# Hybrid attention and RWKV-7 layer on one core: x requested one column set ahead and paced differently, the first block's second half of x loaded among the first transfers

## The chip, the core and the metric

The program runs on one core of one Trainium2 chip. The metric is the time of one execution on the device, in microseconds (us). In the texts PE is the matrix engine TensorE, DVE is VectorE, ACT is ScalarE, POOL is GpSimd, and SP is the engine that here issues nearly all DMAs.

## What is computed

One layer over 4096 tokens of width 1024, all in float32. One input projection of the normalised x feeds two groups of heads; their gated outputs are projected back, added to x, and normalised once more.

```python
xn = rms_norm(x, norm_g, RMS_EPS)
proj = xn @ w_in                          # 1024 -> 4224 columns
o_a = diff_attention(q1, q2, k1, k2, v_a, lam)          # block-causal, 4 heads
o_a = rms_norm(o_a, subln_g) * (1 - lam_init) * silu(g_a)
rwkv_in = token_shift(proj[..., 2048:], shift_mu)
r, k_b, v_b, wd, ad = split(rwkv_in)
y = rwkv7_recurrence(r, decay(wd), k_mod, v_b, kk, a(ad))   # state 64 x 64, 8 heads
o_b = (group_norm(y) + bonus) * silu(g_b)
h = x + concat([o_a, o_b]) @ w_out
out = rms_norm(h, final_g, RMS_EPS)
```

## The kernel before, in words

There are three phases: the projection together with the whole recurrence (some 2135 us of the profiled execution), the attention, and the output projection. The change touches the first phase only.

**Blocks and column sets.** The tokens are cut into eight blocks of 512. For one block x stands transposed in SBUF, as a rounded part `xh` and a remainder `xl`, and the columns of `w_in` go by in sets. Sets of group B (called r: V, two of R, two of K, the LoRA columns, the gate) and sets of group A (called a: V, two of Q, two of K, the gate) are separate runs over a block, in the order r0 a0 r1 a1 r2 a2 r3 r4 r5 r6 r7 a7 a6 a5 a4 a3. The block of x changes eleven times in that list; the last set of a run whose successor has another block carries the number of that block as `nxt`. Each run begins and ends with a token-major set (kind "t": V and the gate); the sets between are feature-major (kind "f").

**A step.** The generator `tile_job` (L340) gives one step per `yield`; a step is `mm3` (L247 to L250), three matmuls of 128x512: high times high, high times low, low times high. A t set is two parts of 16 steps. In `tm_part` (L264) one part computes two groups of 128 tokens, s0 and s0+1, over eight k; s0+1 runs two steps of k behind s0. The eight weight tiles of a t set lie in a ring of eight (`wb`); the second part frees each tile where s0+1 has used it (`release`, L241), and `prep` (L225) at once requests the tile eight places on. In the first run over a set the tile is loaded raw (L212 to L222), split into a high and a low part by ACT and DVE (L236, L237), and stored to `ws_d` (L239); later runs load it from there (L233, 512 KB a tile).

**x of the next block.** A block of x has two halves of 256 tokens, each loaded by two DMAs of 512 KB (`x_load`, L148) into `xv`, of which there are two buffers, so one half at a time. ACT sums the squares and scales (`x_norm`, L157); PE transposes in four groups of eight (`x_trans`, L168), each into a PSUM buffer `pg`, of which there are three that the recurrence shares; ACT writes `xh` (L179) and DVE `xl` (L180). Half 0 of the next block is requested at the start of the last set, normalised at step 10 of its first part, and transposed at steps 1, 4, 7 and 10 of its second part; step 11 requests half 1. Half 1 is normalised at step 4 of the first part of the next set and transposed at steps 6, 8, 10 and 12. `paced` (L322) holds these step numbers. In the first block half 1 is requested after half 0's transposes (L400), since the buffers are the same; after it, `xfree` lets raw weight tiles use the `xv` buffers (as `xr`).

**What sets the order.** PE's order in phase 1 is written by hand: a `tick` after every step advances four side streams of the recurrence (two that prepare a unit of 256 tokens, one for its chain of chunks, one for its output), each by numbers in `W` that tell after how many steps it goes on. A negative number also holds it until the next multiple of four steps. `a8` stands between the product `rk` on POOL (L506) and the matmuls `pbn` that use it (L524). The order of the other engines, SP with its DMAs among them, is made by a scheduler.

Of the kernel before, what the change touches and what calls it, by code (L numbers as in the profile page):

```python
# [27 lines left out]
    xw=2048, cw=512, pl=1, pelat=330, tb=3, pb=3, lag2=2.0, ms=40, a0=2, a1=2, a2=2, a3=2,  # L28
    a4=2, a5=2, a6=2, a7=2, a8=2, a9=2, b0=2, b1=2, b2=2, b3=2, b4=2, b5=2,
    b6=2, b7=2, b8=1, b9=1, c0=10, c1=8, c2=2, c3=2, c4=1, c5=1, c6=2, c7=3,  # L30
# [78 lines left out]
def _phase1(ctx, tc, nc, e):  # L109
# [36 lines left out]
    xraw = {}  # L146

    def x_load(b, t):  # L148
        xs = []
        for s in range(2):  # L150
            r0 = b * BT + t * 256 + s * 128
            xv = xp.tile([128, D], F32, tag="xv", name="xv", bufs=2)
            nc.sync.dma_start(xv, x[r0:r0 + 128, :])
            xs.append(xv)
        xraw[b, t] = xs
# [38 lines left out]
    def raw_next():  # L194
        while True:
# [10 lines left out]
            raw_load(n, raw)  # L206
            wr[n] = raw

    def raw_load(n, raw):
# [53 lines left out]

    def tm_part(n0, s0, evac, last, side_x):  # L264
        po = {}
        order = []
        for n in range(KD + 2):
            if n < KD:
                order.append((s0, n))
            if n >= 2:  # L270
                order.append((s0 + 1, n - 2))
        for s, k in order:
# [67 lines left out]
    def tile_job(i, kind, parts, evs, nxt):  # L340
# [5 lines left out]
        half1 = bg.pop(1, None)  # L346
        assert half1 is None or nxt is None
        if nxt is not None:
            x_load(nxt, 0)
        if half1 is not None:  # L350
            side = paced(x_half1(half1), (4, 6, 8, 10, 12, 13))
        else:
            side = paced(x_norm0(nxt) if nxt is not None else iter(()), (10,))
        yield from tm_part(n0, 0, evs[0], False, side)
        for _ in side:
            pass
        side = paced(x_half0(nxt) if nxt is not None else iter(()), (1, 4, 7, 10, 11))
        yield from tm_part(n0, 2, evs[0], True, side)
        for _ in side:
# [37 lines left out]
    def main():  # L397
        x_norm(0, 0)
        yield from x_trans(0, 0)
        x_load(0, 1)  # L400
        bg[1] = 0
        for _ in range(RING):
            prep()
        for i, (k, parts, evs, nxt, rdone) in enumerate(jobs):
            yield from tile_job(i, k, parts, evs, nxt)
            if rdone:
                done_r[0] += 1
# [1044 lines left out]
```

## Time and profile before

| what | value |
|---|---|
| median of 3 runs | 3769.85 us (3767.56 to 3772.0) |
| the profiled execution | 3761.58 us, span 3759.9 us |
| PE busy | 3609.4 us, 96% of the span |
| DVE, ACT, POOL busy | 70%, 51%, 20% |
| granted PE clock, mean of the span | 0.983 |
| DMA | 593.60 MB, mean 158 GB/s |

An engine is idle before an instruction when that one waits; the profile names who ended the wait. Matmuls are pipelined, so a busy PE is not PE at its peak, but time in which PE waits is lost unless something else bounds the stretch. The granted clock is 1.00 at 2.4 GHz and 0.50 at 1.2 GHz; a stretch of mean 0.76 was thus at the lower level for about half its time.

### The profile page before, as it was taken

How to read it: one execution, taken by the hardware profiler on the slowest of the kernel's cores; microseconds unless marked ns; L12 is line 12 of the kernel's file. 1: busy time of each engine (PE TensorE's matmuls, PEld its weight loads, DVE VectorE, ACT ScalarE, POOL GpSimd, SP SyncE). 2: the span in 40 equal slices, each digit the busy share in tenths (PEclk: the TensorE clock that was granted, in tenths of full speed). 3: DMA queues.
4: the chain of work that ended last, by engine and by line, in shares of the span. 5: the costliest groups of instructions: out<-in, count | busy, mean ns of one | idle time of the engine just before them, and what ended most of it. 6: DMA issues, size and time to landing. Idle time of an engine off the chain costs nothing.

```text
span 3759.9 us, 69957 instructions
## 1 busy us (share of the span) xinstructions
PE 3609.4 (96%) x26370; PEld 3050.9 (81%) x26370; DVE 2632.4 (70%) x5882; ACT 1922.4 (51%) x4042; POOL 761.2 (20%) x1156
## 2 busy tenths in 40 slices
PE   7999999999999999998999999999999999989999
PEld 5777777777777778777777789999999999978887
DVE  3566666667767787757777588898898898863333
ACT  4452352444445443444444377787787787761111
POOL 0112211211212222212221032222222222211000
PEclk9999999999999999999999999999999999999999
DMA  7976665666555565665675651141141131033332
GB/s 231 354 267 204 209 212 198 222 204 225 192 192 190 191 226 174 215 209 196 221 239 200 204 122 48 41 113 37 49 104 49 38 82 40 21 134 121 134 134 74
DMA packets 346092, 593.60 MB, mean 158 GB/s; under 512 B 55193, under 2 KB 210329, under 8 KB 345754
## 3 DMA queue, kind: packets, MB, share of 16 engines
q1 hardware_dynamic: 344602, 587.62, 48.4%
q8 instruction: 208, 3.41, 0.4%
q10 hardware_dynamic: 1152, 1.51, 0.1%
q14 instruction: 130, 1.06, 0.1%
HBM read 434.85 MB, written 154.14 MB: 157 GB/s over the span
## 4 chain that ended last, share of the span: by engine, by line
PE 75%; DVE 13%; DMA 4%; ACT 3%; issue 2%; SPq 2%; POOL 1%; DVEq 0%; POOLq 0%; ACTq 0%
PE po L1222 12%; PE ps L1127 6%; PE ps L1126 6%; PE tp L1197 6%; PE pjf L248 5%; PE pjf L250 4%; PE pjf L249 4%; PE pjt L248 4%; PE pjt L250 4%; PE pjt L249 4%; PE po L1372 3%; PE po L1371 3%; PE po L1370 3%; DVE DG L578 2%; DVE TL L579 2%
## 5 line engine op out<-in xcount | busy, mean ns | idle before, releaser
L1159 ACT ACTIVATE ring<-ring,nm 128x2048 f32<-128x2048 f32 (+14 forms) x472 | 589.0, 1253 | 31.3 <-DVE nm L1151 30.2
L1141 DVE CUSTOM_DVE_ANT_0 ring<-ps,zcol 128x1024 f32<-128x1024 f32 (+6 forms) x464 | 485.2, 1058 | 109.2 <-PE ps L1127 103.1
L1222 PE MATMUL po<-v,pt 128*128 128x128 f32 x4224 | 539.5, 276 | 10.0 <-ACT pt L1210 5.4
L1222 PEld LDWEIGHTS po<-v,pt 128*128 128x128 f32 x4224 | 517.9, 192 | 28.5 <-ACT pt L1210 7.3
L1126 PE MATMUL ps<-k,ta 128*128 128x512 f32 (+3 forms) x1152 | 483.1, 420 | 7.3 <-DMA ta<-q_d 4.9
L248 PE MATMUL pjt<-w,xh 128*128 128x512 f32 x1024 | 436.2, 426 | 29.1 <-DMA w<-ws_d 13.4
L248 PE MATMUL pjf<-xh,w 128*128 128x512 f32 x1088 | 451.1, 415 | 6.0 <-ACT w L236 4.5
L1127 PE MATMUL ps<-k,tb 128*128 128x512 f32 (+3 forms) x1152 | 432.0, 379 | 0.0
L250 PE MATMUL pjf<-xh,w 128*128 128x512 f32 x1088 | 431.0, 396 | 0.5 <-DVE w L237 0.5
L249 PE MATMUL pjf<-xl,w 128*128 128x512 f32 x1088 | 429.9, 395 | 0.0
L249 PE MATMUL pjt<-w,xh 128*128 128x512 f32 x1024 | 410.5, 401 | 0.9 <-DVE w L237 0.9
L250 PE MATMUL pjt<-w,xl 128*128 128x512 f32 x1024 | 410.0, 401 | 0.1
L1182 DVE SCALAR_TENSOR_TENSOR ring<-ring,rho 128x512 f32<-128x512 f32 (+3 forms) x600 | 407.1, 702 | 1.6
L1210 ACT COPY pt<-tp 128x512 f32<-128x512 f32 (+3 forms) x576 | 303.1, 550 | 194.0 <-PE tp L1197 188.7
L1197 PE MATMUL tp<-ident,ring 128*128 128x128 f32 x2112 | 313.6, 274 | 3.7 <-DVE ring L1182 3.7
L1197 PEld LDWEIGHTS tp<-ident,ring 128*128 128x128 f32 x2112 | 254.6, 142 | 40.6 <-issue 3.7
L248 PEld LDWEIGHTS pjt<-w,xh 128*128 128x128 f32 x1024 | 199.0, 194 | 80.9 <-DMA w<-ws_d 20.3
L248 PEld LDWEIGHTS pjf<-xh,w 128*128 128x128 f32 x1088 | 207.3, 191 | 57.4 <-ACT w L236 6.5
L250 PEld LDWEIGHTS pjf<-xh,w 128*128 128x128 f32 x1088 | 207.0, 190 | 49.2 <-DVE w L237 2.7
L1126 PEld LDWEIGHTS ps<-k,ta 128*128 128x128 f32 x1152 | 219.2, 190 | 32.8 <-issue 5.0
L1127 PEld LDWEIGHTS ps<-k,tb 128*128 128x128 f32 x1152 | 220.1, 191 | 23.4
L249 PEld LDWEIGHTS pjf<-xl,w 128*128 128x128 f32 x1088 | 208.0, 191 | 38.1
(205 smaller groups left out, 6421.4 us busy)
## 6 DMA issues: line engine op xcount, KB each, us to landing
w<-ws_d SPq DMA_DIRECT2D x448, 512.0 KB, 5.3
ws_d<-w SPq DMA_DIRECT2D x64, 512.0 KB, 5.3
xv<-in_x_dram SPq DMA_DIRECT2D x48, 512.0 KB, 5.4
ta<-q_d SPq DMA_DIRECT2D x128, 128.0 KB, 2.9
tb<-q_d SPq DMA_DIRECT2D x128, 128.0 KB, 3.0
k<-k_d SPq DMA_DIRECT2D x32, 512.0 KB, 7.1
mi<-mix_d SPq DMA_DIRECT2D x32, 512.0 KB, 3.3
xi<-in_x_dram SPq DMA_DIRECT2D x32, 512.0 KB, 4.2
```

Source lines behind the costliest of these rows:

```text
L248: nc.tensor.matmul(po, ah, bh, start=(k == 0), stop=False)
L249: nc.tensor.matmul(po, ah, bl, start=False, stop=False)
L250: nc.tensor.matmul(po, al, bh, start=False, stop=(k == KD - 1))
L1126: nc.tensor.matmul(ps[:, c:c + w], rr(ta[:, m, qs]), rr(k[:, m, c:c + w]), start=True, stop=False)
L1127: nc.tensor.matmul(ps[:, c:c + w], rr(tb[:, m, qs]), rr(k[:, m, c:c + w]), start=False, stop=True)
L1141: nc.vector.tensor_tensor_reduce(rg(m, ro, x), st["ps", b, m][:, c - 1024 * b:c - 1024 * b + x], msk, 0.125, -3.0e38, ALU.add, ALU.max, ac ...
L1159: nc.scalar.activation(rg(m, ro, x), rg(m, ro, x), AF.Exp, bias=st["nm"][:, m:m + 1], accum_out=st["lp"][:, m, j:j + 1])
L1182: nc.vector.scalar_tensor_tensor(rg(0, ro, x), in0=rg(1, ro, x), scalar=st["rho"], in1=rg(0, ro, x), op0=ALU.mult, op1=ALU.add)
L1197: nc.tensor.transpose(tp[:, j], rg(0, c, 128), ident)
L1210: nc.scalar.copy(pt[:, :n], st.pop(("tp", g))[:, :n])
L1222: nc.tensor.matmul(st["po"], pt[:, j], vt[h, kb // 8][:, kb % 8], start=(kb == 0), stop=(kb == i))
L1370: nc.tensor.matmul(po, mh[:, k], wh[k][:, fs], start=(k == 0), stop=False)
```

## The change

Six edits. (1) The next block's half 0 is requested before the set ahead of the last one, if the last set's weights are not fresh ones; it is then normalised at step 3, else at step 10 as before. (2) Half 0 is transposed at steps 0, 3, 5 and 8 of the second part and half 1 requested at step 9. (3) Half 1 of a later block is normalised at step 5 of the next set and transposed at steps 12, 14, 17 and 20, so the last two groups fall into the second part. (4) In the second part s0+1 runs four k behind s0 where it ran two. (5) The first block's half 1 is requested right after the fourth raw weight tile, into a buffer of the recurrence (`ARF`, first used by it later). (6) `a8` is 5 where it was 2.

```diff
-    a4=2, a5=2, a6=2, a7=2, a8=2, a9=2, b0=2, b1=2, b2=2, b3=2, b4=2, b5=2,
+    a4=2, a5=2, a6=2, a7=2, a8=5, a9=2, b0=2, b1=2, b2=2, b3=2, b4=2, b5=2,
...
-    def x_load(b, t):
+    def x_load(b, t, home=None):
...
-            xv = xp.tile([128, D], F32, tag="xv", name="xv", bufs=2)
+            xv = xp.tile([128, D], F32, tag="xv", name="xv", bufs=2) if home is None else home[:, s]
...
             raw_load(n, raw)
             wr[n] = raw
+            if n == 3:
+                home = rp.tile([128, 4, 4, 2, 64], F32, tag="ARF", name="xv1", bufs=2)
+                x_load(0, 1, home.rearrange("p (s a) b c d -> p s (a b c d)", s=2))
...
-    def tm_part(n0, s0, evac, last, side_x):
+    def tm_part(n0, s0, evac, last, side_x, lag):
...
-        for n in range(KD + 2):
+        for n in range(KD + lag):
             if n < KD:
                 order.append((s0, n))
-            if n >= 2:
-                order.append((s0 + 1, n - 2))
+            if n >= lag:
+                order.append((s0 + 1, n - lag))
...
+        if half1 is not None:
+            side = paced(x_half1(half1), (5, 12, 14, 17, 20, 21) if half1 else (4, 6, 8, 10, 12, 13))
+        elif nxt is not None:
+            if (nxt, 0) not in xraw:
+                x_load(nxt, 0)
+                side = paced(x_norm0(nxt), (10,))
+            else:
+                side = paced(x_norm0(nxt), (3,))
+        else:
+            side = iter(())
+        yield from tm_part(n0, 0, evs[0], False, side, 2)
         if nxt is not None:
-            x_load(nxt, 0)
-        if half1 is not None:
-            side = paced(x_half1(half1), (4, 6, 8, 10, 12, 13))
-        else:
-            side = paced(x_norm0(nxt) if nxt is not None else iter(()), (10,))
-        yield from tm_part(n0, 0, evs[0], False, side)
-        for _ in side:
-            pass
-        side = paced(x_half0(nxt) if nxt is not None else iter(()), (1, 4, 7, 10, 11))
-        yield from tm_part(n0, 2, evs[0], True, side)
+            for _ in side:
+                pass
+            side = paced(x_half0(nxt), (0, 3, 5, 8, 9))
+        yield from tm_part(n0, 2, evs[0], True, side, 4)
...
-        x_load(0, 1)
         bg[1] = 0
...
+            if i + 1 < len(jobs) and jobs[i + 1][3] is not None and not tiles[min(first_tile[i + 1], len(tiles) - 1)][3]:
+                x_load(jobs[i + 1][3], 0)
             yield from tile_job(i, k, parts, evs, nxt)
```

Three places show what this does to the engines' orders. The first is **SP at the start of the program**, before: `xv_213` and `xv_215` are half 1 of the first block, and the first `xr` tiles (L222) come 23 places after it, behind the small constants and the first loads of the recurrence.

```order
L239 DMA ws_d_70<-w_245 128x1024
L140 DMA lng_519<-in_ln_x_g_dram 64x256
L140 DMA lnb_522<-in_ln_x_b_dram 64x256
L153 DMA xv_213<-in_x_dram 128x1024
L153 DMA xv_215<-in_x_dram 128x1024
L140 DMA lnb_522<-in_ln_x_b_dram 64x256
L135 DMA w0h_525<-in_w0_dram 64x4x1 x2
```

And of the change (its lines are numbered from 1 to 9 higher; `xv1_139`, half 1, now stands eighth, between the fourth and the fifth raw tile):

```order
L242 DMA ws_d_70<-w_236 128x1024
L140 DMA lnb_521<-in_ln_x_b_dram 64x256
L242 DMA ws_d_70<-w_240 128x1024
L242 DMA ws_d_70<-w_244 128x1024
L225 DMA xr_351<-in_w_in_dram 128x2x64 x8
L225 DMA xr_360<-in_w_in_dram 128x2x64 x7
L317 DMA vb_d_67<-st_336 128x512
```

The first 15 of the `xr` requests moved up, directly behind the stores of the first eight tiles and ahead of most constants.

The second is **SP where block 3 gives way to block 4** (the end of r3 and the start of r4), before: `xv_8635` and `xv_8637` are half 1 of block 4, `xv_9787` and `xv_9789` are already half 0 of block 5, `w` are weight tiles, `st` evicted results. Of the eight tiles of the new set, four are requested ahead of half 1 (the last of them is the first row), four behind it.

```order
L233 DMA w_8616<-ws_d_70 128x1024
L153 DMA xv_8635<-in_x_dram 128x1024
L153 DMA xv_8637<-in_x_dram 128x1024
L233 DMA w_8633<-ws_d_70 128x1024
L233 DMA w_8649<-ws_d_70 128x1024
L233 DMA w_8654<-ws_d_70 128x1024
L314 DMA gb_d_68<-st_8642 128x512
L233 DMA w_8663<-ws_d_70 128x1024
L314 DMA gb_d_68<-st_8659 128x512
L153 DMA xv_9787<-in_x_dram 128x1024
L314 DMA vb_d_67<-st_8879 128x512
L153 DMA xv_9789<-in_x_dram 128x1024
```

And of the change (`xv_8626` is half 1 of block 4, `xv_9698` and `xv_9700` half 0 of block 5):

```order
L236 DMA w_8605<-ws_d_70 128x1024
L153 DMA xv_8624<-in_x_dram 128x1024
L153 DMA xv_8626<-in_x_dram 128x1024
L236 DMA w_8622<-ws_d_70 128x1024
L236 DMA w_8638<-ws_d_70 128x1024
L236 DMA w_8643<-ws_d_70 128x1024
L317 DMA gb_d_68<-st_8631 128x512
L236 DMA w_8648<-ws_d_70 128x1024
L236 DMA w_8653<-ws_d_70 128x1024
L236 DMA w_8662<-ws_d_70 128x1024
L317 DMA gb_d_68<-st_8658 128x512
L317 DMA vb_d_67<-st_8812 128x512
```

Only two of the eight tiles now stand ahead of half 1, six behind it; half 0 of block 5 comes three rows after the last one shown, behind one more store and one load of the recurrence. It was requested a block early before the change too.

The third is **PE at the end of phase 1**, before. `pc` and `py` are the recurrence's last chunk, `pjt` the last column set, `ps` (in the change) the attention's first matmuls.

```order
L716 MATMUL pc_21437<-svu_21376,bkt_20520 64x64 x8
L721 MATMUL py_21367<-svu_21376,GS_20519 64x64 x8
L248 MATMUL pjt_21430<-w_21253,xh_123 128x512
L249 MATMUL pjt_21430<-w_21253,xh_123 128x512
L250 MATMUL pjt_21430<-w_21253,xl_124 128x512
L248 MATMUL pjt_21441<-w_21227,xh_123 128x512
```

Eight more matmuls of the column set follow there, then the attention. In the change:

```order
L253 MATMUL pjt_21418<-w_21218,xl_124 128x512
L704 MATMUL pc_21461<-xs_21488,TT1_583 64x64 x8
L711 MATMUL py_21399<-svu_21408,ARF_19478 64x64 x8
L725 MATMUL pc_21461<-svu_21408,bkt_20558 64x64 x8
L730 MATMUL py_21399<-svu_21408,GS_20557 64x64 x8
L1135 MATMUL ps_21646<-k_21636,ta_21630 128x128
```

The recurrence runs eight steps later throughout (four at the very end), so the last column set ends first, and half of the last chunk stands alone behind it.

## Rows read from the trace of the kernel before

**Rows 1.** The page's part 1: busy us (share of the span) and instructions of each engine.

```profile
PE 3609.4 (96%) x26370; PEld 3050.9 (81%) x26370; DVE 2632.4 (70%) x5882; ACT 1922.4 (51%) x4042; POOL 761.2 (20%) x1156
```

**Rows 2.** Waits of PE in phase 1: waiter <- whom: us, times, longest.

```profile
PE pt L176 <- ACT xv L166: 38.9, 19, 9.7
PE pjt L248 <- DMA w<-ws_d: 13.4, 12, 2.9
PE pbn L524 <- POOL rr L506: 13.3, 3, 5.2
PE pt L176 <- DVE xl L180: 11.9, 5, 4.5
PE pjt L248 <- DVE st L311: 11.7, 7, 4.0
```

**Rows 3.** Stretches: length, busy us (count) of each engine, granted PE clock, DMA share, GB/s.

```profile
30.00:45.00 15.00, 7.66 (x33) 6.15 (x34) 7.16 (x22) 10.53 (x23) 3.47 (x6) 0.77 0.41 110
512.00:530.00 18.00, 15.32 (x60) 12.43 (x59) 15.98 (x38) 13.17 (x28) 4.45 (x7) 0.72 0.27 93
770.00:785.00 15.00, 12.32 (x52) 9.86 (x52) 13.63 (x34) 12.32 (x26) 3.91 (x5) 0.77 0.23 93
890.00:904.00 14.00, 14.00 (x180) 11.49 (x179) 6.26 (x13) 10.05 (x25) 0.00 (x0) 1.00 0.94 348
1279.00:1300.00 21.00, 15.21 (x162) 11.90 (x161) 14.20 (x29) 12.00 (x27) 3.50 (x3) 0.76 0.67 218
1398.00:1412.00 14.00, 8.81 (x75) 7.02 (x76) 9.30 (x17) 8.43 (x20) 3.42 (x3) 0.76 0.47 162
1612.00:1630.00 18.00, 14.39 (x63) 11.24 (x62) 15.59 (x40) 15.17 (x33) 5.63 (x7) 0.81 0.37 116
```

**Rows 4.** Timeline of PE, transposes of the first block: start, us, instruction [idle before].

```profile
11.80 2.18 PE L176 MATMUL pt<-ident,xv 128*128 128x128 f32 x9 [1.18 <-ACT xv L166]
33.39 0.55 PE L176 MATMUL pt<-ident,xv 128*128 128x128 f32 x3 [4.26 <-ACT xv L166]
37.89 0.48 PE L176 MATMUL pt<-ident,xv 128*128 128x128 f32 x1 [3.95 <-ACT xv L166]
```

**Rows 5.** Waits of PE between 70 and 120 us.

```profile
PE pjf L248 <- ACT w L236: 4.5, 4, 1.9
PE pjt L248 <- ACT w L236: 3.2, 2, 2.8
```

**Rows 6.** Timeline of PE, SP and ACT from 760 to 775 us, block 2 to block 3.

```profile
760.60 0.60 PE L176 MATMUL pt<-ident,xv 128*128 128x128 f32 x4
761.12 0.81 SPq L153 DMA_DIRECT2D xv<-in_x_dram  x2
771.73 0.33 PE L176 MATMUL pt<-ident,xv 128*128 128x128 f32 x1 [0.38 <-ACT xv L166]
773.14 1.16 ACT L166 ACTIVATE xv<-xv,rs 128x1024 f32<-128x1024 f32 x1
774.36 0.33 PE L176 MATMUL pt<-ident,xv 128*128 128x128 f32 x1 [2.30 <-ACT xv L166]
```

**Rows 7.** Timeline of PE and DVE, a transposed group and its first remainder, unhindered.

```profile
1899.81 0.60 PE L176 MATMUL pt<-ident,xv 128*128 128x128 f32 x4
1900.96 0.48 DVE L180 SCALAR_TENSOR_TENSOR xl<-pt,g_t,xh 128x256 fp32r<-128x256 f32 x1 [0.32 <-ACT xh L179]
```

**Rows 8.** Weight requests (L233) from 895.2 to 897.7 us, just behind an x half.

```profile
DMA to landing us min/median/max: 8.6/9.3/9.9
```

**Rows 9.** The page's part 6, weight tiles in all: KB each, median us to landing.

```profile
w<-ws_d SPq DMA_DIRECT2D x448, 512.0 KB, 5.3
```

**Rows 10.** Timelines of DVE, SP and PE at the end of phase 1.

```profile
2132.66 0.87 DVE L728 TENSOR_TENSOR svu<-svu,WC 64x256 f32<-64x256 f32 x2
2134.10 0.59 SPq L1033 DMA_DIRECT2D ta<-q_d  x1
2140.38 0.73 PE L1126 MATMUL ps<-k,ta 128*128 128x512 f32 x1 [4.87 <-DMA ta<-q_d]
```

## The prediction, made blind

> **What bounds the kernel now.** I read the page's part 1 first: PE is busy for 96% of the span, DVE for 70% [rows 1]. So time is won only where PE waits or runs at its lower clock. Next the list of PE's waits in phase 1 [rows 2]: five kinds carry 89.2 us. The largest is a transpose of x waiting for ACT to scale it (38.9 us); then weight tiles that have not landed (13.4), `pbn` waiting for the product on POOL (13.3), a transpose waiting for DVE's `xl`, that is for a PSUM buffer (11.9), and a token-major group waiting for DVE's eviction of an earlier one (11.7). Then the stretches around such waits, for the clock [rows 3]: it is 0.72 to 0.81 around six of them, and the loss is length times (1 - clock). From 512 to 530 us that is 18 x 0.28 = 5.0 us, more than PE stood still there. Last the timelines, for why each wait is there.
>
> Of the 38.9 us, 9.7 (the longest) and 1.2 are the start of the program [rows 2, 4], which the change leaves. 4.3 + 3.9 = 8.2 belong to the first block's half 1 [rows 4]. The other 19.8 lie at the changes of block. One of them in full [rows 6]: half 0's last transposes end at 761.20; half 1 is requested at 761.12, and its second tile is scaled at 774.30, 13.2 us later. PE comes to its transposes after 12 steps, at 771.35 (a step there is 10.15 / 12 = 0.85 us), and stands 0.4 + 2.3 us.
>
> **The change, part by part.** The sum is made against the profiled execution's own 3761.58 us, which is 8.3 us below the median of the runs shown; the same saving is taken from that median at the end.
>
> *First block's half 1 among the first transfers.* Its transposes now follow 16 steps of matmuls without a stop: -8.2 us [rows 4], and the clock of that stretch, 15 x 0.23 = 3.4 us [rows 3]: **-11.6**. What hides the earlier request: raw tiles five to eight come behind 1 MB more, 3.0 us later at the 348 GB/s of a stretch with the DMA engines 94% busy [rows 3]. PE uses the fifth tile only six steps after its first one, and its first transposes end no sooner than 13.98 [rows 4], so I cost that at 0, and at 3 if those steps don't cover it. The `xr` requests move up by as many places as the constants take, so they do not fall behind PE's lead; the waits of 7.7 us for split weights between 70 and 120 us [rows 5] could vanish or double. Bounds: -27 (they vanish, with the clock beside them) to -4 (they double).
>
> *Half 1 at the later changes of block.* From half 0's last transposes (step 8 of the second part, before step 10) to half 1's first (step 12 of the next set, before step 6) there are now 20 steps where 12 stood: 20 x 0.85 = 17.0 us against the 13.2 that request, landing and scaling take [rows 6]. So the 19.8 us go, with the clock of the three stretches where they cost most: 18 x 0.28 + 15 x 0.23 + 18 x 0.19 = 11.9 us [rows 3]. I credit nine tenths of 31.7: **-29**. Bounds: -32 to -15 (three quarters of the waits, and no clock).
>
> *`a8` from 2 to 5.* With the multiple of four it holds to, this is mostly four steps, 4 x 0.85 = 3.4 us, taken off each of the three waits: 13.3 - 10.2 leaves 3.1 [rows 2]. The two stretches cost 21 x 0.24 + 14 x 0.24 = 8.4 us of clock [rows 3]; three quarters of that go: 10.2 + 6.4 = **-16.6**. Bounds: -22 to 0 (the wait moves with the matmuls, since DVE is what is late).
>
> *Four k of distance instead of two.* The second group of a part needs an old group's PSUM buffer three steps later, so the waits for DVE's eviction, 11.7 us in seven [rows 2], lose some 3 x 0.85 = 2.5 us each at most; half of the total: **-6**. Bounds: -11.7 to 0.
>
> *Half 0 at steps 0, 3, 5, 8 and normalised earlier*: 0, its scaling was early enough already, and the 11.9 us for `xl` [rows 2] stay: three PSUM buffers and one step less between the first and the fourth group. Bounds: +9 (0.85 at eleven changes) to -12.
>
> *The request one set ahead* I cost at 0: in SP's order the next block's half 0 already stands right behind half 1's transposes, a whole block early; the two orders shown above differ by two stores that now go before it.
>
> **What the change adds.** *(a)* Two of half 1's four groups are transposed inside the second part, which uses them. The fifth k is used two steps after its transposes (2 x 0.85 = 1.7 us); the unhindered way through ACT and DVE takes 1901.44 - 1900.41 = 1.0 us [rows 7], so nothing is lost when DVE is free, and up to 4.5 when it comes as late as for `xl` at worst [rows 2]. Bounds 0 to 11 x 4.5 = 50; nearest is the mean of those five waits, 2.4 us, at perhaps a third of eleven changes: **+8**. *(b)* Weight tiles are freed later (steps 5, 7, 9, 11 to 15 of the second part, not 3, 5, 7 and on), and six of eight now stand behind half 1 on SP. The third is freed at step 9 and used 9 steps later, 7.7 us at 0.85 a step. Tiles requested just behind an x half landed after 9.3 us [rows 8] against 5.3 for all [rows 9]. 1.6 us late at eleven changes would be 18; but most steps carry work of the recurrence (phase 1 has 2112 steps in some 2135 us, about 1.0 us each), and at 1.0 it is 0.3. Bounds 0 to 18: **+5**. Behind a late tile on SP stand stores, with four buffers. *(c)* The end: the recurrence ends after the last column set instead of inside it. The attention's loads wait for its last state (`svu` done at 2133.53, first load at 2134.10) [rows 10]. Behind the last projection matmul now stand alone two passes of the recurrence through PE and three pairs on DVE of about 0.87 us, one of which is the row; I take 5 us with the ways between. Some 2 us of matmuls that moved behind it are not lost, but a stop longer than the 4.87 us of before brings clock, and the next tiles of Q now queue behind an output's loads: **+7**. Bounds +3 to +14.
>
> Sum: -11.6 - 29 - 16.6 - 6 + 8 + 5 + 7 = -43. DVE, busy at 70%, must do the same in less time, and some of PE's gaps were its slack; I hand back 5: **-38**, 3723.6 in the profiled execution's terms, 3769.85 - 38 = **3732** in the runs'.
>
> A rule that speaks against (b) stands in the Trainium skill, page "DMA: Bandwidth & Descriptors", section "Queues, rings and completion order": on each DMA engine, descriptors of a queue are consumed in ring order. By that alone a tile behind x waits for all of x, and the row of 9.3 us agrees with it; the sum with every change of block charged 1.6 us for it would be 13 us higher.
>
> **The rivals.**
> *Late weight tiles take the place of late x (slower).* Place: tiles three to eight of each new set. Tile three is wanted 7.7 us after its release and lands 9.9 after it at worst [rows 8], 2.2 late; those behind it are freed and wanted at the same distance. At eleven changes that is 24 us, and a stop of such a size has cost 3.4 us of clock (15 x 0.23 for 0.4 + 2.3) [rows 3, 6], 37 more: +61 against the -48 of all else: +13, 3783. It decides from 48 / 11 = 4.4 us a change, the clock included. For: the rows of 8.6 to 9.9 us, the later release. Against: with four tiles behind x the waits for tiles were 13.4 us in twelve in the whole phase [rows 2].
> *DVE is the next limit.* The waits for scaled x become waits for `xh` and `xl` in the second part, and `pbn` keeps waiting. For: DVE's lateness of 4.5 us [rows 2]; against: it is free for 30% of the span [rows 1]. Then (a) is +25 and `a8` 0: -43 + 17 + 17 = -9, 3761.
> *Everything hidden.* x, `pbn`, evictions and the start's split weights stop waiting, and the clock stays up: -27 - 32 - 22 - 12 + 7 = -86, 3684. For: each wait has its edit. Against: DVE's part in 11.9 + 11.7 us [rows 2].
> *It does not do what it says.* The scheduler asked for x a block early before, and may give half 1's scaling a place on ACT as late as its transposes: only the first block gains, and the end costs: -11.6 + 7 = -5, 3765. Against: the 13.2 us are almost all transfer and arithmetic, not waiting [rows 6].
>
> **How the numbers follow.** Forecast 3732 with 0.60 (its own range 3710 to 3750), everything hidden 0.12, DVE next 0.13, late tiles 0.09, no effect 0.06. The range, 3694 to 3764, takes in the forecast, half of everything hidden, DVE next, and some of no effect; left out are the late tiles and the halves. A measurement here can tell about 0.2%, 7.5 us, from no change. Faster: the forecast, everything hidden, and 0.08 of DVE next, which lies on that edge: 0.80. Same: the rest of it and most of no effect: 0.10. Slower: late tiles and a little of the last: 0.10.
>
> **What would show it.** The wait of transposes for scaled x falls from 38.9 to about 12 us, all at the start; no transposes wait at 30 to 40 us; `pbn` waits 3 us or less; the granted clock over the span rises above 0.985; new small waits of the projection for `xl` or `xh`; a longer stop of PE before the attention (4.87 before). I am wrong if waits for weight tiles grow beyond 30 us, or if those for DVE grow by what x gives back.

## The result, and the profile after

The changed kernel is **slower**: 3796.66 us (median of 4 runs, 3789.94 to 3799.88) against 3768.7 (median of 4, 3767.39 to 3772.0), ratio 1.0071, 95% interval [1.0053, 1.0088]. Taken again beside other kernels on one chip: 3794.72 against 3771.73, 1.0059 [1.0047, 1.0071]. The profiled execution took 3789.94 us, 28.4 above that of before. The page's part 1 of the changed kernel, beside [rows 1]:

```profile
PE 3616.8 (95%) x26370; PEld 3053.5 (81%) x26370; DVE 2633.6 (70%) x5882; ACT 1917.2 (51%) x4042; POOL 764.3 (20%) x1156
```

The engines do the same work: PE is busy 7.4 us more in a span 27.9 us longer, at a mean granted clock of 0.976 (0.983 before), so it stands still 20.5 us longer. Next PE's waits in the changed kernel, from the start to 2170 us (waiter <- whom: us, times, longest; lines are 3 to 9 higher than before):

```profile
PE pjt L251 <- DMA w<-ws_d: 26.9, 23, 3.2
PE pt L176 <- ACT xv L166: 14.3, 3, 9.7
PE pjt L253 <- DVE xl L180: 10.5, 10, 2.0
PE pt L176 <- DVE xl L180: 9.1, 4, 4.1
PE pjt L251 <- ACT w L239: 8.9, 3, 4.9
PE pjt L251 <- DVE st L314: 8.3, 3, 3.9
...
PE pjf L251 <- ACT w L239: 6.0, 6, 2.1
PE pa L467 <- DVE xl L180: 5.8, 3, 2.8
PE pjt L251 <- DVE sl L304: 5.2, 1, 5.2
```

The five kinds of [rows 2] fell from 89.2 us to 58.6: the waits for scaled x from 38.9 to 14.3 (10.9 of it at the start), those of `pbn` from 13.3 to none. These two went as they were meant to. But waits for weight tiles doubled, and kinds came that [rows 2] does not have: the third matmul of a step waiting for `xl`, `pa` for a PSUM buffer that `xl` holds, a group of the projection for `sl` on DVE, and the recurrence's `ptt` for `Zs` on ACT (4.8 us). Summed over all rows of the two lists, PE's waits for DVE rose from 41.9 to 65.1 us, for ACT other than scaled x from 12.2 to 26.8, and for DMAs from 19.8 to 36.8.

Where the time was lost shows in a table by stretch. Both kernels are cut at the same steps of the projection: step 64 ends the first row, then 128, 640, 1152, and the last row begins at step 2112 (columns as in [rows 3]). Before:

```profile
0.00:73.90 73.90, 54.45 (x225) 43.62 (x226) 29.07 (x73) 35.96 (x69) 9.30 (x28) 0.95 0.72 222
73.90:135.50 61.60, 52.46 (x193) 38.15 (x192) 22.70 (x46) 18.78 (x34) 3.84 (x3) 0.92 0.96 331
135.50:621.50 486.00, 466.54 (x3459) 377.91 (x3457) 322.14 (x715) 201.69 (x449) 88.39 (x88) 0.99 0.69 233
621.50:1132.80 511.30, 490.42 (x3952) 396.80 (x3953) 337.73 (x751) 218.44 (x490) 104.03 (x106) 0.98 0.62 207
...
2134.70:3759.90 1625.20, 1591.51 (x10434) 1423.15 (x10432) 1209.97 (x2728) 1022.10 (x2042) 329.75 (x710) 0.99 0.28 81
```

And of the change:

```profile
0.00:62.80 62.80, 50.32 (x225) 40.98 (x226) 24.19 (x59) 30.70 (x62) 5.42 (x25) 1.00 0.80 254
62.80:132.20 69.40, 54.96 (x193) 39.05 (x192) 28.15 (x57) 22.33 (x40) 8.28 (x6) 0.85 0.90 299
132.20:634.50 502.30, 473.14 (x3459) 380.85 (x3457) 312.67 (x694) 201.69 (x450) 89.92 (x88) 0.97 0.65 225
634.50:1158.90 524.40, 494.58 (x3945) 398.57 (x3946) 338.20 (x762) 214.57 (x486) 99.44 (x104) 0.97 0.60 202
...
2155.70:3787.80 1632.10, 1595.82 (x10498) 1426.34 (x10497) 1212.23 (x2734) 1022.74 (x2043) 330.95 (x710) 0.99 0.27 81
```

The start gains 73.9 - 62.8 = 11.1 us and gives 7.8 back in the next 64 steps, at a clock of 0.85 where 0.92 stood. Then 16.3 and 13.1 us are lost over five changes of block, at 0.97 where 0.99 and 0.98 stood: PE stands still 9.7 and 8.9 us longer there and is busy 6.6 and 4.2 longer. The last row, attention and all, is 6.9 longer. (In the two rows left out, from step 1152 to 1600 and on to 2112, the change is 10.8 us shorter and 5.7 longer.) One caution on all single traces here: the executions of the kernel before, 11 to 35 beside each group of experiments, spread over 3755.8 to 3780.1 us in all, so small differences are read from medians.

### The profile page after: what moved, and what is told of

It is laid out like the page before. It is cut to its first block, busy times and chain, and to the rows that moved or that the text cites. A ratio compares the mean times of both kernels' runs of the same rounds, so it can differ in the third digit from the quotient of the medians.

```text
span 3787.8 us, 69962 instructions
## 1 busy us (share of the span) xinstructions
PE 3616.8 (95%) x26370; PEld 3053.5 (81%) x26370; DVE 2633.6 (70%) x5882; ACT 1917.2 (51%) x4042; POOL 764.3 (20%) x1156
## 3 DMA queue, kind: packets, MB, share of 16 engines
q10 hardware_dynamic: 1152, 1.51, 0.1%
## 4 chain that ended last, share of the span: by engine, by line
PE 64%; DVE 11%; DMA 4%; issue 2%; ACT 2%; POOL 1%; SPq 0%; DVEq 0%; POOLq 0%; ACTq 0%
PE po L1231 12%; PE ps L1136 6%; PE ps L1135 6%; PE tp L1206 6%; PE pjt L251 3%; PE po L1381 3%; PE po L1380 3%; PE po L1379 3%; PE pjt L253 3%; PE pjt L252 3%; PE pjf L251 3%; PE pjf L253 2%; PE pjf L252 2%; DVE TL L588 1%; DMA w<-ws_d 1%
## 5 line engine op out<-in xcount | busy, mean ns | idle before, releaser
L251 PE MATMUL pjt<-w,xh 128*128 128x512 f32 x1024 | 441.9, 432 | 59.5 <-DMA w<-ws_d 26.9
L253 PE MATMUL pjt<-w,xl 128*128 128x512 f32 x1024 | 416.4, 408 | 10.5 <-DVE xl L180 10.5
L252 PE MATMUL pjt<-w,xh 128*128 128x512 f32 x1024 | 415.9, 406 | 0.8 <-DVE w L240 0.8
L253 PEld LDWEIGHTS pjt<-w,xl 128*128 128x128 f32 x1024 | 201.1, 196 | 62.1 <-DVE xl L180 16.4
```

Of the source, the lines that this page charges most:

```text
L251: nc.tensor.matmul(po, ah, bh, start=(k == 0), stop=False)
L252: nc.tensor.matmul(po, ah, bl, start=False, stop=False)
L253: nc.tensor.matmul(po, al, bh, start=False, stop=(k == KD - 1))
```

## The experiments

The changed kernel and the one before are called "after" and "before". Ratios are to runs of before in the same rounds, with the 95% interval.

| kernel | median us | before, us | ratio |
|---|---|---|---|
| before + edit 5 (early x of the first block) | 3775.92 | 3771.38 | 1.0014 [1.0005, 1.0023] |
| before + edit 6 (`a8`) | 3778.05 | 3770.31 | 1.0020 [1.0009, 1.0032] |
| before + edit 4 (four k) | 3768.99 | 3770.31 | 0.9997 [0.9987, 1.0008] |
| before + edits 1 to 3 (x's pace) | 3772.24 | 3770.31 | 1.0006 [0.9995, 1.0017] |
| before + edits 1 to 4 | 3770.90 | 3771.73 | 1.0002 [0.9993, 1.0011] |
| after, edit 6 undone | 3771.12 | 3771.38 | 1.0002 [0.9992, 1.0012] |
| after, half 1's pace undone | 3773.51 | 3771.38 | 1.0004 [0.9993, 1.0015] |
| after, edit 4 undone | 3779.28 | 3771.38 | 1.0022 [1.0011, 1.0033] |
| after, edit 5 undone | 3798.60 | 3771.52 | 1.0069 [1.0057, 1.0081] |
| after | 3794.72 | 3771.73 | 1.0059 [1.0047, 1.0071] |
| before, x of later blocks not loaded | 3769.48 | 3770.31 | 0.9995 [0.9987, 1.0004] |
| before, no `xl` of later blocks | 3767.26 | 3771.73 | 0.9991 [0.9982, 1.0001] |
| after, no `xl` of later blocks | 3764.40 | 3771.73 | 0.9976 [0.9968, 0.9985] |
| after, three passes of y left out on DVE | 3762.88 | 3766.91 | 0.9986 [0.9976, 0.9995] |
| after, 27 us more on DVE | 3793.32 | 3771.52 | 1.0059 [1.0044, 1.0074] |
| before, folded `norm_g` | 3770.02 | 3766.91 | 1.0005 [0.9997, 1.0014] |
| after, folded `norm_g` | 3769.66 | 3766.91 | 1.0006 [0.9997, 1.0015] |
| before + edits 1 to 4, folded `norm_g` | 3759.55 | 3766.91 | 0.9986 [0.9976, 0.9995] |

**One edit undone.** Three theories: weight tiles come late because of edit 4; the recurrence, moved by `a8`, meets the projection badly; half 1's groups in the second part wait for DVE.

```diff
-        yield from tm_part(n0, 2, evs[0], True, side, 4)
+        yield from tm_part(n0, 2, evs[0], True, side, 2)
```

> The changed kernel with the distance between the two token groups of the second part put back from four k to two; everything else as changed. Theory 'late tiles' (the distance holds each weight tile two steps longer, and six of eight tiles now stand behind half 1 of x on SP): the projection's waits for stored tiles fall from 26.9 to about 15 us, the new waits of mm3's third matmul for DVE's xl (10.5) stay or grow by 2, and with the clock around the tile waits the time falls by 15 to 25 us, to about 3775. Theory 'recurrence moved' (the eight-step shift by a8 makes the loss): tile waits within 4 us of 27, time within 6 us of the change (3797). Theory 'half 1 in the second part': the xl waits and the wait of pa for xl stay at about 16 us, time at most 8 us lower.

```diff
-    a4=2, a5=2, a6=2, a7=2, a8=5, a9=2, b0=2, b1=2, b2=2, b3=2, b4=2, b5=2,
+    a4=2, a5=2, a6=2, a7=2, a8=2, a9=2, b0=2, b1=2, b2=2, b3=2, b4=2, b5=2,
```

> The changed kernel with a8 put back from 5 to 2, so that the recurrence's streams stand against the projection as they did before; everything else as changed. Theory 'recurrence moved': the waits of pbn for POOL return (about 13 us), but the new waits of ptt, pc for svu, and the eviction waits near step 1984 go (some 12 us), the stop before the attention falls from 6.97 to about 4.9 us with 5 us of clock, and in sum 15 to 30 us come back: 3767 to 3782. Theory 'late tiles' or 'half 1 in the second part': tile waits stay at 27 and xl waits at 16, only the tail's 7 us come back and pbn's 13 return: 3797 to 3803.

```diff
-            side = paced(x_half1(half1), (5, 12, 14, 17, 20, 21) if half1 else (4, 6, 8, 10, 12, 13))
+            side = paced(x_half1(half1), (4, 6, 8, 10, 12, 13))
```

> The changed kernel with half 1 of the later blocks back at steps 4, 6, 8, 10, 12 and 13 of the next set, so that all four of its groups are transposed within the first part; everything else as changed. Theory 'half 1 in the second part': the new waits of mm3's third matmul for xl (10.5 us) and of pa for xl (5.8) go; the waits of transposes for scaled x return only in part, 5 to 12 us, since half 1 is requested two steps earlier than before the change; time 3775 to 3785. Theory of the prediction (the pace is worth 29 us): the x waits come back in full, about 20 us more than now with their clock, time 3815 to 3825. Theory 'late tiles' or 'recurrence moved': within 6 us of 3797.

Each theory's own run gave about the time it had foretold: any of the three edits undone brings 15 to 24 us of after's 3794.72 back. So none of the three is the cause alone; most of the loss needs all of them. With `a8` put back the waits of `pbn` returned (8.9 us), and those for `sl` and for ACT's `Zs` went. The waits of the other two runs are the more telling part. With edit 4 undone, the waits of PE are (the first three of that kernel's list):

```profile
PE pjt L251 <- DVE st L314: 26.9, 11, 7.3
PE pt L176 <- ACT xv L166: 14.3, 3, 9.7
PE pjt L251 <- DMA w<-ws_d: 13.7, 18, 3.4
```

The tile waits halved as expected, and the waits for an eviction by DVE rose by 18.6 us. With half 1's pace undone the waits for `xl` in the third matmul went, and tile waits rose instead (the first two of its list):

```profile
PE pjt L251 <- DMA w<-ws_d: 32.9, 23, 3.6
PE pt L176 <- ACT xv L166: 20.4, 10, 9.9
```

From this came the theory "waits are handed on": PE, spared one wait, arrives earlier at the next producer that is no earlier than it was. By part 1 of their pages (span less busy time) PE stands still as long in these two as in after: 169.6 us with edit 4 undone and 172.1 with half 1's pace undone, against 171.0 (150.5 before). It is busy 9.4 and 13.8 us less for the same instructions, at a mean clock of 0.981 against 0.976. So in these single traces what came back is time at the higher clock, not stops.

**One edit alone.** The start first.

```diff
+            if n == 3:
+                home = rp.tile([128, 4, 4, 2, 64], F32, tag="ARF", name="xv1", bufs=2)
+                x_load(0, 1, home.rearrange("p (s a) b c d -> p s (a b c d)", s=2))
...
-        x_load(0, 1)
```

> The kernel before with edit 5 alone: half 1 of the first block is requested behind the fourth raw weight tile, into the recurrence's buffer. The prediction credited this with 11.6 us, kept to the end: about 3757. Theory 'taken back by the raw weights' (progress in the changed kernel was 11 us ahead at step 64 and 3 us at step 128, with the DMA engines 1.05 busy from 100 to 130 us): 8 of the 11 us are lost again before step 128, as the waits for split raw weights between 70 and 125 us grow from 7.7 to about 14 us; the time is 0 to 5 us below the kernel before, 3764 to 3769.

It is 4.5 us slower, worse than both values expected. The waits for split raw weights rose from 7.7 us [rows 5] to

```profile
PE pjt L251 <- ACT w L239: 8.6, 3, 4.0
PE pjf L251 <- ACT w L239: 7.1, 6, 2.1
```

The table by stretch suggests why the lead does not last: up to step 128 both kernels move the same bytes (222 x 73.9 + 331 x 61.6 = 36.8 MB against 254 x 62.8 + 299 x 69.4 = 36.7), mostly fresh weights, in 135.5 and 132.2 us. That the bytes bound the stretch is argued and not shown: the DMA engines are busy for 0.72 and 0.96 of its two parts before, 0.80 and 0.90 after. Undone in after (the same lines the other way), edit 5 changes nothing that the intervals show (1.0069 against 1.0059 and 1.0071), and neither value expected for it held:

> The changed kernel with the first block's half 1 requested after half 0's transposes again, as before. It cost 4.5 us alone, so by the theory of DVE's time 3785 to 3793. By the theory of an unlucky alignment that any edit leaves: 3770 to 3780.

`a8` alone:

> The kernel before with edit 6 alone (a8 from 2 to 5). The prediction's term: -16.6 us (bounds -22 to 0), about 3755, from 10.2 us less waiting of pbn and 6.4 of clock. Theory 'waits are handed on' (in the first four experiments time times clock moved by less than 6 us, while every kind of wait that an edit was made for did shrink): pbn's 13.3 us go, but the recurrence now meets the projection eight steps later, where ptt, pc and the token-major groups wait for ACT and DVE instead, and the stop before the attention grows by some 2 us: within 6 us of the kernel before, and rather above than below.

It costs 7.7 us where 16.6 were to be won. `pbn` no longer waits, but the recurrence now comes upon other work:

```profile
PE pt L176 <- ACT xv L166: 46.6, 22, 10.0
PE pjt L248 <- DVE st L311: 20.5, 9, 5.5
...
PE pjt L248 <- DVE sl L301: 5.5, 1, 5.5
PE ptt L613 <- ACT Zs L599: 5.3, 2, 3.1
```

Evictions wait 8.8 us more, scaled x 7.7 more, `sl` and `Zs` are new, and the end has its longer stop (6.6 us, 4.87 before).

Four k of distance alone, and x's pace alone (edits 1 to 3):

> The kernel before with edit 4 alone (four k between the two groups of the second part). The prediction's terms for it: -6 from evictions and +5 from later weight tiles, so 3770. Theory 'waits are handed on': the waits for DVE's eviction fall from 11.7 to about 5 us, those for stored weight tiles rise from 13.4 to about 20, time within 5 us of the kernel before. Theory 'late tiles' (the first experiment gave 18 us back for this edit in the changed kernel): tile waits rise to 25 and the time by 10 us or more.

> The kernel before with edits 1 to 3 alone (half 0 requested a set ahead and normalised at step 3, its groups at 0, 3, 5, 8; half 1 of later blocks at 5, 12, 14, 17, 20). The prediction's terms: -29 for half 1 and +8 for its groups in the second part: about 3750. Theory 'waits are handed on': the 19.8 us of transposes waiting for scaled x at the changes of block go to under 3, but waits of the projection for xl and xh (some 10 us), of pa for xl's PSUM buffer (3 to 6) and for weight tiles (8 more) take their place: 3765 to 3775.

Each edit is the lines of the change itself, and neither measures as a difference. With edit 4 alone:

```profile
PE pjt L248 <- DMA w<-ws_d: 21.9, 21, 3.3
...
PE pjt L248 <- DVE st L311: 3.3, 2, 2.2
```

Evictions 8.4 us less, tiles 8.5 more. With x's pace alone the waits for scaled x are 22.4 us, gone but for 1.5 and the first block's 20.9, and there stand in their place

```profile
PE pjt L250 <- DVE xl L180: 8.7, 6, 2.8
PE pjt L248 <- ACT xh L179: 8.5, 5, 2.6
```

**Is x late because it is loaded late?** The prediction had said so of [rows 6].

```diff
     def x_load(b, t):
+        if xkeep:
+            xraw[b, t] = xkeep
+            return
...
         xraw[b, t] = xs
+        if b > 0:
+            xkeep.extend(xs)
```

> The kernel before, with x of the later blocks not loaded: every block after the first half of block 1 scales and transposes what lies in the two x buffers, so 28 loads of x at the changes of block (28 of 512 KB or a few more) are left out and nothing else. If the waits for scaled x and for tiles behind x are what the time hangs on, 20 us of x waits, some 6 of tile waits and 12 of clock go: about 3733. Theory 'waits are handed on': x waits fall to under 6 us and the time by at most 12 us, to 3759 or more, since DVE, ACT and the weight tiles stop PE in the same stretches.

(In fact 42 of the 48 loads are gone.) The time is the same, and so are the waits for scaled x: 37.1 us. Both theories had them fall, and both missed. Here is the change of block of [rows 6] in this kernel, the timeline of PE, its waiting transposes:

```profile
776.54 0.33 PE L183 MATMUL pt<-ident,xv 128*128 128x128 f32 x1 [0.36 <-ACT xv L173]
...
779.17 0.76 PE L183 MATMUL pt<-ident,xv 128*128 128x128 f32 x3 [2.29 <-ACT xv L173]
```

0.36 and 2.29 us, where 0.38 and 2.30 stood with the transfers. ACT's timeline tells what they wait for:

```profile
771.06 0.65 ACT L538 COPY BON<-pbn 64x4 f32<-64x4 f32 x4
771.74 0.60 ACT L169 ACTIVATE jk<-xv 128x512 f32<-128x512 f32 x1
...
775.34 1.15 ACT L173 ACTIVATE xv<-xv,rs 128x1024 f32<-128x1024 f32 x1 [0.51 <-POOL rs L92]
776.51 0.84 ACT L474 ACTIVATE lw<-pw,w0h 128x256 f32<-128x256 f32 x2
777.24 0.84 ACT L482 ACTIVATE tha<-pa,a0h 128x256 f32<-128x256 f32 x2
777.95 1.16 ACT L173 ACTIVATE xv<-xv,rs 128x1024 f32<-128x1024 f32 x1
```

x has long been there. ACT begins the squares when it is done with `BON`, and the second scaling stands behind `lw` and `tha` of the recurrence. It is ACT's order that makes x late. (With the transfers ACT waited 0.28 us for the first tile at this place, after the same `BON`.) The Trainium skill, page "TensorE: Matmul & The Clock Gate", section "Architectural detail: the array is 16× 32×32, not 1× 128×128", says of these engines "ACT/DVE are strict FIFO"; the trace agrees: the scaling's data were ready and it waited for its turn. And the tile waits (16.2 us here, 13.4 before) are no smaller with 22 MB less on the queue, so in the kernel before it is not x in front of them that makes PE wait for tiles. Where [rows 8] has 9.3 us to landing, tiles requested from 895.9 us on land after 6.3 here (5.5 to 6.8); PE waited for none of them in either kernel. After was not run without x.

**Who takes the gain?** `xl` was the largest new name in after's waits, so DVE was relieved of it, in both kernels: the remainder of the later blocks is left out (block 0's stays): 176 passes, 192 - 16 (the expectation has 160).

```diff
-                nc.vector.scalar_tensor_tensor(xl[:, k, ts], in0=pt[:, kk], scalar=g_t[:, k:k + 1], in1=fr(xh[:, k, ts]), op0=ALU.mult, op1=ALU.subtract)
+                if b == 0:
+                    nc.vector.scalar_tensor_tensor(xl[:, k, ts], in0=pt[:, kk], scalar=g_t[:, k:k + 1], in1=fr(xh[:, k, ts]), op0=ALU.mult, op1=ALU.subtract)
```

> The changed kernel itself, on the chip of the other runs of this call, to have its difference from the kernel before in the same rounds as theirs: 20 to 28 us above the kernel before. Time times mean clock was 3708 for it in four executions and 3696 to 3697 for the kernel before: if both parts are real, 10 us more at full clock and 10 to 16 us more of clock.

> The changed kernel without the remainder xl of the later blocks (xl stays that of block 0), which takes 176 - 16 = 160 passes of 0.48 us, 77 us, off DVE at the changes of block and nothing off PE. Theory 'DVE takes the gain' (edits that let PE come earlier at a change of block turn into waits for DVE): the waits for xl (10.5 + 9.1 + 5.8 us) and some for evictions go, with clock, and the time falls by 35 to 55 us, below the kernel before without xl. Theory 'tiles and ACT's order': the waits for stored weight tiles (27) and for ACT stay, only some 15 to 25 us go, and the distance to the kernel before without xl stays at about 20 us.

> The kernel before without the remainder xl of the later blocks. Theory 'DVE takes the gain': its waits of transposes for xl (11.9) go and some of those for evictions, 10 to 20 us with the clock, 3750 to 3760; the waits for scaled x (38.9) stay, since no edit of the change is made. Theory 'tiles and ACT's order': 10 to 20 us as well. The two kernels without xl are told apart by their distance: changed below before by the first, above by about 20 us by the second.

After fell by 30.3 us, less than "DVE takes the gain" had foretold (35 to 55) and more than "tiles" (15 to 25). Before fell by 4.5 (its interval touches 1), where both had 10 to 20. After's median is now the lower of the two (3764.40 against 3767.26; the intervals of the ratios just overlap), although its tile waits even rose, to

```profile
PE pjt L252 <- DMA w<-ws_d: 37.4, 30, 5.1
```

So the loss goes while the tile waits stay, and DVE's passes have a part in it. Is it `xl`'s place, or DVE's work as such? Three passes of the output stream were left out instead (the centring of y, its scale by `lng`, the added bonus), with `xl` as it was:

```diff
-            nc.vector.scalar_tensor_tensor(g8(yv), in0=nm.unsqueeze(2).broadcast_to([128, 8, 64]), scalar=1.0 / 64, in1=g8(yv), op0=ALU.mult, op1=ALU.add)
...
-            nc.vector.tensor_tensor(yv, yv, lng.unsqueeze(1).broadcast_to([128, 2, 256]), ALU.mult)
...
-            nc.vector.tensor_tensor(yv, yv, bv, ALU.add)
```

> The changed kernel without three passes of the recurrence's output stream on DVE (96 of 0.69 us, 66 us; the centring, the scale and the added bonus of y are left out), xl as in the changed kernel. If DVE's work in general takes the gain, about as much comes back as for xl's 77 us, some 25 us: 3768 to 3775. If it is xl's own place (the third matmul of a step and a PSUM buffer wait for it), the waits for xl stay above 15 us and the time falls by less than 10 us, to 3785 or more.

The time came back nearly as fully as without `xl` (1.0059 to 0.9986), while the waits for `xl` stayed (22.7 us, 25.4 in after):

```profile
PE pjt L253 <- DVE xl L180: 9.7, 9, 2.0
PE pt L176 <- DVE xl L180: 8.3, 3, 4.2
...
PE pa L467 <- DVE xl L180: 4.7, 3, 3.0
```

So it need not be `xl`'s place (before was not run without these passes): by part 1 of their pages DVE is busy 2556.3 us here and 2563.7 without `xl`, 77 and 70 us less than in after. But the amount of DVE's work alone it is not either: with `a8` put back DVE is busy 2637.9 us, no less than in after (2633.6), and the time came back in full. The counter-test added work:

```diff
+            for _ in range(2):
+                nc.vector.tensor_copy(yv, yv)
             nc.vector.tensor_tensor(yv, yv, bv, ALU.add)
```

> The changed kernel with two copies of yv onto itself ahead of the bonus in the recurrence's output stream: 64 passes more on DVE, some 0.45 us each, 29 us, and nothing else. By the theory that the changed kernel is short of DVE's time (64 to 77 us less gave 31 back) it gets 5 to 15 us slower: 3800 to 3810 beside a kernel before of 3771. By the theory of an unlucky alignment that any edit leaves: 3770 to 3785.

The 64 copies are there, 27.0 us in the groups of that kernel's DVE:

```profile
L785 DVE COPY yv<-yv 128x512 f32<-128x512 f32 x64 | 27.0, 422 | 1.2
```

and the time did not rise (1.0059, as after). The expectation of 5 to 15 us missed, though with six executions the interval does not exclude some 5 us. It also speaks against the other theory, that after is an unlucky alignment which any edit mends: this edit did not mend it, nor did edit 5 undone. A milder form, that after's streams meet badly and most edits move them, is not excluded. What follows is only that relief helps; there is no price per us of DVE work.

**A cheaper `xh` and `xl`.** `norm_g` is multiplied into the weights when they are split, so one pass of 512 columns does for two of 256; the result is the same.

```diff
-            for kk in range(2):
...
+            k = slice(2 * k2, 2 * k2 + 2)
+            nc.scalar.copy(xh[:, k, ts], pt)
+            nc.vector.tensor_tensor(xl[:, k, ts], pt, fr(xh[:, k, ts]), ALU.subtract)
...
+        for hi, lo, src, k in parts:
+            nc.scalar.activation(hi, src, AF.Copy, scale=g_t[:, k:k + 1])
+            nc.vector.scalar_tensor_tensor(lo, in0=src, scalar=g_t[:, k:k + 1], in1=fr(hi), op0=ALU.mult, op1=ALU.subtract)
```

> The kernel before with the same folding. Without xl altogether it lost 3 us; with a quarter of that it should lose at most 3, and the start may lose a few us to the second pass of each feature-major tile: 3765 to 3775.

> The changed kernel with norm_g folded into the weights as they are split, so that xh and xl need one pass of 512 columns where they needed two of 256: ACT has 88 passes of about 0.58 us for 176 of 0.47, DVE 88 of 0.69 for 176 of 0.48; the 34 feature-major raw tiles take two passes instead of one, some 10 us more on each in the first 240 us. By the theory that DVE's passes for xl take the gain, 23 of 83 us of them less give about 23/77 of the 31 us, 9, and ACT's 30 us some more: 3778 to 3786. By the theory of xl's place alone, within 6 us of the changed kernel, 3788 to 3798.

> The kernel before with edits 1 to 4, without the early x of the first block and without a8. Those two alone cost 4.5 and 7.7 us, and the changed kernel with a8 put back stood at the kernel before: if the start's cost adds up, this is 3 to 6 us below the kernel before; if the edits hinder each other in pairs, it is within 4 us of it or above.

> Edits 1 to 4 without the early x and without a8, with the same folding. These edits stood at the kernel before (3771); they remove 17 us of waits for scaled x and leave 26 us of waits for xl. If half as many passes shorten those by a third, with the clock, 3755 to 3763, below both kernels; if the waits for stored weight tiles (25) take their place, 3765 to 3773.

Before gains nothing by it, as expected. After gains more than expected: from 1.0059 to 1.0006. The relief is small: over the span DVE is busy 11.1 us less than in after and ACT 14.5, since the splits take more passes. So this run does not tell DVE's part from ACT's. And edits 1 to 4, which were worth nothing (1.0002), are now worth 0.14%: 3759.55 us, the fastest kernel here, with nothing left out, below before by an interval that does not touch 1, below before with the same folding by 10.5 us, and below after by more. It lies under the 0.2% that the prediction called tellable, but 11 runs against 33 tell it. DVE's groups with L179 in that kernel:

```profile
L179 DVE TENSOR_TENSOR xl<-pt,xh 128x512 fp32r<-128x512 f32 x96 | 65.3, 688 | 54.2 <-ACT xh L178 53.2
```

and before:

```profile
L180 DVE SCALAR_TENSOR_TENSOR xl<-pt,g_t,xh 128x256 fp32r<-128x256 f32 x192 | 89.8, 479 | 58.2 <-ACT xh L179 57.0
```

## Why the prediction was wrong

It said 3732 us, faster with 0.80; it was 3796.66, outside the range. By its own steps:

- **The start, -11.6.** Right to step 64 (-11.1), wrong after it: that the lead lasts was taken for granted, and "-4 (they double)" was not the worst end. The waits for split weights went from 7.7 to 14.9 us in after (8.9 + 6.0), the clock of the 64 steps behind from 0.92 to 0.85. Alone it measured +4.5.
- **Half 1, -29.** The waits went as foretold (19.8 to 14.3 - 10.9 = 3.4 us), but the step that read [rows 6] was wrong: "request, landing and scaling take" 13.2 us. Without the transfer the stops at that place are the same to 0.02 us; ACT's order sets them. That the waits went all the same is in part luck: twenty steps instead of twelve leave time for ACT's order as well as for a transfer. And none of it was time won: edits 1 to 3 alone are 1.0006.
- **`a8`, -16.6.** `pbn`'s 13.3 us went in full; the price was new waits of about 27 us for evictions, scaled x, `sl` and `Zs` in the run with `a8` alone. Its bounds ended at 0, so a loss was in no case. It measured +7.7. (Three quarters of 8.4 are 6.3, so the term was -16.5.)
- **Four k, -6, and (b), +5.** Right in sum: -8.4 and +8.5 us of waits, nothing measured. But the reason given for (b), tiles behind x, is at most a part of it: in before with x not loaded PE waits 16.2 us for tiles, and in after its two longest waits for a tile (3.23 us at 382.43 us, 2.96 at 758.69) come over 100 us after the last load of x. Waits up to 16 us behind a load of x make 13.3 of after's 26.9 us. What the ring order that the prediction cited costs in after no run here shows.
- **(a), +8.** It was 10.5 + 5.8 us of such waits, twice the term. (2.4 us at a third of eleven changes are 8.8.)
- **(c), +7.** Right: 1632.10 - 1625.20 = 6.9 us from step 2112 on. The attention's first full matmul comes 12.0 us after that step (2167.73 - 2155.70) where 5.7 stood (2140.38 - 2134.70): 2.1 us of longer stop, and the rest is the half chunk that now stands alone, as foretold.

```profile
2167.73 0.77 PE L1135 MATMUL ps<-k,ta 128*128 128x512 f32 x1 [6.97 <-DMA ta<-q_d]
```

- **The hand-back, +5: the step that failed.** "DVE, busy at 70%, must do the same in less time, and some of PE's gaps were its slack; I hand back 5." Four savings were added up as if each wait removed were time won, with 5 us off for all of them. But the waits went and the time did not: the edits alone measured +4.5, +1.9, -1.3 and +7.7 us (edit 5, edits 1 to 3, edit 4, edit 6) where -11.6, -21, -1 and -16.6 stood. The sign that the prediction had named came true: PE's waits for DVE grew by 23.2 us, and x gave back 24.6. With 70 to 77 us taken off DVE all of the 23 us and a little more came back (0.9976 and 0.9986). The rival "DVE is the next limit", at 0.13, was the nearest in kind, though it ended at 3761. Its counter-argument, that DVE is free for 30% of the span, compared means: in the three stretches of [rows 3] at changes of block DVE was busy 15.98 of 18 us, 13.63 of 15 and 15.59 of 18, that is 89%, 91% and 87%. In the two around `pbn`, at 1279 and 1398 us, it was busy for 68% and 66%, so there a share does not explain the price of `a8`.
- **The clock.** It was to rise above 0.985 and fell to 0.976. In the second measurement of after the executions' mean was 0.9778 against 0.9804 for before: by length times (1 - clock), 0.0026 x 3794 = 10 of the 23 us lost are clock, the other 13 more stops. That a removed stop gives its clock back was counted in three terms, 3.4, 11.9 and 6.4 us. With those edits alone the executions' mean clock went from 0.9803 to 0.9803 (edit 5), from 0.9803 to 0.9809 (edits 1 to 3, some 2 us) and from 0.9803 to 0.9793 (`a8`, some 4 us lost).

What stays open: why edits 3, 4 and 6 cost some 20 us together while no two of them do (1.0002, 1.0004 and 1.0022 with one undone), why more work on DVE then costs nothing that shows, and whether relief of ACT alone, or after without x's loads, would have ended the loss too; neither was run. Shown is that undoing any one of the three, or taking work off DVE, ends it or most of it.

## What to carry to other kernels

Where PE is busy for 96% of the time and its waits are spread over a dozen producers, a wait removed is not a gain: ask which producer PE meets next, and read that engine's busy share in the stretch of the wait, not over the span. Try each edit alone before they are added up. Before a wait for data is put down to the transfer, look at the consumer's engine: what stands between the data's landing and the instruction in that engine's order? And where one engine is near its limit in those stretches, making its passes fewer may come first: here the re-pacing that was worth nothing (1.0002) was then worth 10.5 us.

## What was not expected of the hardware

One pass of DVE over 512 columns of a PSUM group takes 688 ns where two over 256 take 2 x 479 = 958, and one of ACT 582 where two take 2 x 472. These are different instructions, with the scale in the short ones and without it in the long, so they do not price the columns. The folded kernel runs one instruction at both widths, in the weights' splits: from 256 to 512 columns DVE's goes from 507 to 749 ns and ACT's from 505 to 722. By that, as an estimate, some 265 ns of a short pass on DVE and 290 on ACT are not columns. Leaving out 42 loads of 512 KB changed the time by nothing that shows (0.9995) and did not lower the waits for weight tiles (16.2 us against 13.4). The waits that ACT had for `xl` before its next `xh` (50.6 us in before) are not among those of the folded kernel, where ACT waits there for PE (60.2 of 60.6 us):

```profile
L178 ACT CAST xh<-pt 128x512 fp32r<-128x512 f32 x96 | 54.6, 582 | 60.6 <-PE pt L176 60.2
```
